# FiLM layer: the stores moved from ACT's DMA queue to SP's, behind the loads

## Chip, cores, metric

One core of a Trainium2 chip. The metric is device time in microseconds (us), lower is better. The span in a profile is about 1.8 us shorter than the time. Most executions agree within 0.3%; some are 1.5% to 5% longer, and these slow ones are left out of all comparisons. MB is 10^6 bytes, except in the profile's KB column.

## The reference

```python
# x: (32, 512, 256) f32, conditioning: (32, 64), gamma_proj and beta_proj: (64, 256)
gamma = conditioning @ gamma_proj
beta = conditioning @ beta_proj
return (x * (1 + gamma[:, None, :]) + beta[:, None, :]).astype(np.float32)
```

16.78 MB of x are read, 16.78 MB of output are written; the rest is small.

## The kernel before

x goes through SBUF in four slabs of 4.19 MB, each with its own buffer (nothing is ever reused, so no load waits for a store). Each slab is worked on in two groups of 16 rows per partition: 11 rows on VectorE, 5 on GpSimd, a multiplication and an addition each, in place. Each group is then stored, so there are eight stores, called S0 to S7 below.

```python
    LOADS = {0: [8, 24]}
    GROUP = 16
    ON_DVE = 11
    ...
    nc.scalar.dma_start(out=cond_s, in_=conditioning)
    nc.scalar.dma_start(out=gbproj[:, :dim], in_=gamma_proj)
    nc.scalar.dma_start(out=gbproj[:, dim:], in_=beta_proj)
    ...
    for s in range(SLABS):
        xs = xpool.tile([P, ROWS, dim], f32, name=f"xs{s}")
        ...
        for n in LOADS.get(s, [ROWS]):
            nc.sync.dma_start(out=xs[:, r : r + n, :], in_=x_v[s, :, r : r + n, :])
    ...                       # gamma and beta for each partition by matmuls: gb_p (PSUM), gb_s (SBUF)
    for s in range(SLABS):
        for r0 in range(0, ROWS, GROUP):
            ...
            nc.vector.scalar_tensor_tensor(out=v, in0=rows(g_p, nv), scalar=1.0, in1=v,
                                           op0=ALU.add, op1=ALU.mult)
            nc.gpsimd.tensor_tensor(out=w, in0=w, in1=rows(g_s, nw), op=ALU.mult)
            nc.vector.tensor_add(out=v, in0=v, in1=rows(b_p, nv))
            nc.gpsimd.tensor_tensor(out=w, in0=w, in1=rows(b_s, nw), op=ALU.add)
            nc.scalar.dma_start(out=o_v[s, :, r0 : r0 + GROUP, :],
                                in_=xs[:, r0 : r0 + GROUP, :])
```

## Time and profile before

| | before |
|---|---|
| time, median (range) | 84.53 us (84.4 to 85.89, 6 runs) |
| span of the profiled run | 82.6 us |
| bytes, mean rate over the span | 33.69 MB, 408 GB/s |
| VectorE / GpSimd busy | 60% / 56% |
| last VectorE instruction ends | 66.6 us |
| first store issued, last load landed | 25.9 us, 49.5 us |

The chain of work that ended last (shares of the span by engine):

```profile
DVE 49%; DMA 16%; issue 11%; PE 2%; ACTq 1%; ACT 1%
```

### The profile page before, as it was taken

What the parts mean: (1) busy time and instruction counts of PE and PEld (TensorE: products, weight loads), DVE (VectorE), ACT (ScalarE), POOL (GpSimd) and SP (SyncE); (2) the same over time, 40 slices, a digit from 0 to 9 for tenths busy, and PEclk for the clock granted to TensorE, in tenths of its full rate; (3) what the DMA queues carried; (4) which work ended last, traced back from release to release, by engine and by line L of the source; (5) the groups of instructions that cost most, each with busy time, mean ns of one, the idle gap of its engine ahead of it and who ended that gap; (6) DMA issues with size and microseconds to landing.
All of it is one profiled execution on the core that took longest, in us unless ns stands there. A gap on an engine that the chain in (4) does not pass through costs nothing.

```text
span 82.6 us, 156 instructions
## 1 busy us (share of the span) xinstructions
PE 9.1 (11%) x10; PEld 2.8 (3%) x10; DVE 49.9 (60%) x18; ACT 3.9 (5%) x9; POOL 46.2 (56%) x22
## 2 busy tenths in 40 slices
PE   0080000899600000000000000000000000000000
PEld 0100000443000000000000000000000000000000
DVE  2011000059999999999999999999999920000000
ACT  0600000034400000000000000000000000000000
POOL 2000000069999999999999999999995000000000
DMA  3899999969969989998889979899999999999992
GB/s 56 337 508 397 389 397 524 460 302 508 508 270 492 508 381 381 413 476 381 381 381 556 460 302 460 381 468 421 429 452 389 468 421 421 460 389 452 437 421 87
DMA packets 2080, 33.69 MB, mean 408 GB/s; under 512 B 288, under 2 KB 416, under 8 KB 416
## 3 DMA queue, kind: packets, MB, share of 16 engines
q1 hardware_dynamic: 720, 16.78, 48.6%
q10 hardware_dynamic: 1360, 16.92, 48.0%
HBM read 16.92 MB, written 16.78 MB: 408 GB/s over the span
## 4 chain that ended last, share of the span: by engine, by line
DVE 49%; DMA 16%; issue 11%; PE 2%; ACTq 1%; ACT 1%
DVE xs L100 30%; DVE xs L103 19%; DMA gbproj<-in_beta_proj_dram 16%; PE gb_p L79 2%; ACTq L50 1%; ACTq L48 0%; ACT gb_s L82 0%; ACT gb_s L85 0%
## 5 line engine op out<-in xcount | busy, mean ns | idle before, releaser
L102 POOL TENSOR_TENSOR xs<-xs,gb_s 128x1280 f32<-128x1280 f32 x8 | 23.0, 2895 | 16.2 <-ACT gb_s L82 16.2
L100 DVE SCALAR_TENSOR_TENSOR xs<-gb_p,xs 128x2816 f32<-128x2816 f32 x8 | 24.7, 3083 | 10.9 <-ACT gb_s L85 10.9
L103 DVE TENSOR_TENSOR xs<-xs,gb_p 128x2816 f32<-128x2816 f32 x8 | 24.7, 3086 | 0.3
L104 POOL TENSOR_TENSOR xs<-xs,gb_s 128x1280 f32<-128x1280 f32 x8 | 23.0, 2893 | 0.0
L79 PE MATMUL gb_p<-gbproj,cond_T 64*128 64x512 f32 x8 | 7.2, 1074 | 8.9 <-DMA gbproj<-in_beta_proj_dram 8.9
L74 DVE COPY cond_T<-cond_T_p 64x512 f32<-64x512 f32 x1 | 0.7, 683 | 4.3 <-PE cond_T_p L72 4.3
L79 PEld LDWEIGHTS gb_p<-gbproj,cond_T 64*128 64x128 f32 x8 | 2.5, 328 | 13.7 <-issue 13.7
L72 PE MATMUL cond_T_p<-rident,cond_s 32*64 32x512 f32 x2 | 1.9, 1065 | 3.9 <-DMA cond_s<-in_conditioning_dram 3.9
L82 ACT ACTIVATE gb_s<-gb_p 128x256 f32<-128x256 f32 x4 | 1.5, 383 | 16.4 <-PE gb_p L79 16.4
L85 ACT COPY gb_s<-gb_p 128x256 f32<-128x256 f32 x4 | 1.5, 367 | 0.0
L82 ACT ACT_TABLE_LOAD x1 | 1.3, 1283 | 2.4 <-issue 2.4
L67 DVE COPY rident<-ident 32x512 f32<-32x512 f32 x1 | 0.4, 416 | 1.2 <-POOL ident masks.py:199 1.2
L72 PEld LDWEIGHTS cond_T_p<-rident,cond_s 32*64 32x64 f32 x2 | 0.3, 202 | 3.9 <-issue 3.9
masks.py:197 POOL MEMSET ident<- 32x32 f32 x1 | 0.1, 114 | 0.3 <-POOLq L121 0.3
masks.py:199 POOL TENSOR_SCALAR_AFFINE_SELECT ident<-ident 32x32 f32<-32x32 f32 x1 | 0.2, 202 | 0.1
L121 POOL MEMSET const-float32-0.0<- 128x1 f32 x1 | 0.1, 103 | 0.2 <-issue 0.2
L121 POOL MEMSET const-bfloat16-1.0<- 128x1 bf16 x1 | 0.1, 106 | 0.0
L121 POOL MEMSET const-uint8-127<- 128x1 uint8 x1 | 0.1, 106 | 0.0
L121 POOL MEMSET const-float32-1.0<- 128x1 f32 x1 | 0.1, 103 | 0.0
## 6 DMA issues: line engine op xcount, KB each, us to landing
out_dram<-xs ACTq DMA_DIRECT2D x8, 2048.0 KB, 18.2
xs<-in_x_dram SPq DMA_DIRECT2D x3, 4096.0 KB, 32.9
xs<-in_x_dram SPq DMA_DIRECT2D x1, 3072.0 KB, 12.2
xs<-in_x_dram SPq DMA_DIRECT2D x1, 1024.0 KB, 4.6
gbproj<-in_gamma_proj_dram ACTq DMA_DIRECT2D x1, 64.0 KB, 9.1
gbproj<-in_beta_proj_dram ACTq DMA_DIRECT2D x1, 64.0 KB, 12.9
cond_s<-in_conditioning_dram ACTq DMA_DIRECT2D x1, 8.0 KB, 3.0
```

Source lines behind the costliest of these rows:

```text
L50: nc.scalar.dma_start(out=gbproj[:, :dim], in_=gamma_proj)
L67: nc.vector.tensor_copy(out=rident.rearrange("p (b g) -> p b g", g=REP), in_=ident.to_broadcast([batch, batch, REP]),)
L72: nc.tensor.matmul(cond_T_p, lhsT=cond_s, rhs=rident, start=True, stop=True)
L74: nc.vector.tensor_copy(out=cond_T, in_=cond_T_p)
L79: nc.tensor.matmul(p_t, lhsT=cond_T[:, s * P : (s + 1) * P], rhs=gbproj, start=True, stop=True)
L82: nc.scalar.activation(out=s_t[:, :dim], in_=p_t[:, :dim], func=mybir.ActivationFunctionType.Identity, bias=1.0, scale=1.0)
L85: nc.scalar.copy(out=s_t[:, dim:], in_=p_t[:, dim:])
L100: nc.vector.scalar_tensor_tensor(out=v, in0=rows(g_p, nv), scalar=1.0, in1=v, op0=ALU.add, op1=ALU.mult)
L102: nc.gpsimd.tensor_tensor(out=w, in0=w, in1=rows(g_s, nw), op=ALU.mult)
L103: nc.vector.tensor_add(out=v, in0=v, in1=rows(b_p, nv))
L104: nc.gpsimd.tensor_tensor(out=w, in0=w, in1=rows(b_s, nw), op=ALU.add)
L121: nc = _bacc.Bacc("TRN2", target_bir_lowering=False, num_devices=1)
```

## The change

Intent: loads first, stores after them, in one queue, so that the loads are never slowed by stores sharing their turns. In the profile SP's queue is q1 and ACT's is q10; a queue's part on one of the 16 DMA engines is called a ring below.

```diff
-            nc.scalar.dma_start(out=o_v[s, :, r0 : r0 + GROUP, :],
-                                in_=xs[:, r0 : r0 + GROUP, :])
+            nc.sync.dma_start(out=o_v[s, :, r0 : r0 + GROUP, :],
+                              in_=xs[:, r0 : r0 + GROUP, :])
```

## The prediction

> **What bounds the kernel now.** I read the page's slices first, because the kernel does two vector passes over 16.78 MB and must read and write each byte once, so the question is whether the DMA engines or VectorE set the end.
>
> ```profile
> DVE  2011000059999999999999999999999920000000
> POOL 2000000069999999999999999999995000000000
> DMA  3899999969969989998889979899999999999992
> DMA packets 2080, 33.69 MB, mean 408 GB/s; under 512 B 288, under 2 KB 416, under 8 KB 416
> q1 hardware_dynamic: 720, 16.78, 48.6%
> q10 hardware_dynamic: 1360, 16.92, 48.0%
> ```
>
> VectorE and GpSimd work without a gap in the middle of the span and stop with seven slices to go. The DMA row is at eight or nine tenths nearly everywhere from the second slice to the last but one. The two queue shares add to 96.6% of all 16 engines' time. By the sizes in the packet records, q1 holds the five loads of x (SP), and q10 the stores together with the three small loads of ACT (16.78 + 0.14 MB).
>
> The chain of work that ended last names VectorE for 49% of the span. That must not be read as the bound: it follows the last store back to the instruction that allowed it. What VectorE's pace is worth shows in the stretches (columns: window, its length, busy time of each engine with instruction counts, clock, DMA share, GB/s):
>
> ```profile
> 2.00:25.90 23.90, 9.09 (x10) 2.79 (x10) 9.03 (x4) 3.87 (x9) 8.60 (x4) 1.00 0.99 418
> 25.90:49.50 23.60, 0.00 (x0) 0.00 (x0) 23.46 (x9) 0.00 (x0) 23.60 (x10) 1.00 1.01 425
> 49.50:80.00 30.50, 0.00 (x0) 0.00 (x0) 16.98 (x6) 0.00 (x0) 13.47 (x5) 1.00 1.01 432
> ```
>
> I chose the borders from the issues: the first store is issued at 25.94 us, and the last load, issued at 10.3 us, lands 39.2 us later, at 49.5. So the first stretch carries loads only, the second both directions, the third stores only. All three move nearly the same, 418, 425 and 432 GB/s, with the engines' share at about 1. Transfers bind in all of them, whatever their direction. After VectorE's last instruction (63.49 + 3.09 = 66.58 us) there are still 16 us of stores: VectorE finished long before the data did.
>
> ```profile
> 63.49 3.09 DVE L103 TENSOR_TENSOR xs<-xs,gb_p 128x2816 f32<-128x2816 f32 x1
> L59 SPq DMA_DIRECT2D xs<-in_x_dram x5: 328/424/623, 0.7 to 10.3; - x5
> L105 ACTq DMA_DIRECT2D out_dram<-xs x8: 338/339/368, 25.9 to 66.7; - x8
> out_dram<-xs ACTq DMA_DIRECT2D x8, 2048.0 KB, 18.2
> ```
>
> A store takes 18.2 us (median) from issue to landing, though 2.10 MB at 432 GB/s need 4.85 us: stores already stand in a backlog, and the compute is not what they wait for.
>
> **What the Trainium skill says.** All from the page "DMA: Bandwidth & Descriptors". "Issuing engines are not separate DMA queues": transfers from any issuing engine run on the same 16 DMA engines, and using several saves only sequencer time. The before trace agrees in that SP's queue alone already gets 418 GB/s, and the two queues together only 425. "Queues, rings and completion order": SP and ACT each own one ring on each of the 16 engines, and an engine takes turns between rings packet by packet. The trace agrees in the split: by 25.9 us about 10.11 MB have moved (418 GB/s for 23.9 us, plus 0.116 MB in the first slice), so 16.92 - 10.11 = 6.81 MB of loads remained and took the 23.6 us to 49.5, that is 289 GB/s, leaving 425 - 289 = 136 for stores. This is 2.1 to 1; load packets are mostly 32 KB and store packets 16 KB in the records, so alternate turns give 2 to 1. "Where 436 GB/s comes from" puts the port ceiling at 435.2 GB/s. The stores-only stretch runs at 432, so nothing is left above it.
>
> **The change part by part.** The order of instructions of the built kernels is the same on PE, VectorE and GpSimd. The eight stores leave ACT and stand on SP behind all five loads.
>
> *Issue time.* Eight stores by 0.339 us = 2.7 us move from ACT to SP. ACT's last compute was at 22.2 us, and SP issues its last load long before 25.9, so both have idle time: 0 us on the path. The fifth load waited until 10.3 us before, for a semaphore shared with the gamma load; in the built kernel after, it shares none and should be issued by about 2.6 us. Four loads stood ahead of it in the queue anyway (8.4 MB not yet moved at 10.3 us is certain, since only some 3.6 MB had), so 0 us too.
>
> *Loads no longer share turns with stores.* From 25.9 us the remaining 6.81 MB of loads have the engines alone: 6.81 MB / 432 GB/s = 15.8 us, so the last load lands at 41.7 us, not 49.5. Nobody waits for it: VectorE has no gap before either. 0 us on the path by itself.
>
> *Stores wait behind the loads.* The first is issued at 25.9 us but moves from 41.7 us. Eight stores are 16.78 MB / 432 = 38.8 us, so the last byte moves at 80.5 us. For this to hold, each store must be ready when its turn comes. Store k (0 to 7) has its turn at 41.7 + 4.85 k; VectorE completes group k at about 23.73 + 6.12 k (L103 ends at 23.73 for the first, 66.58 for the last). Production is slower than the drain, so the slack shrinks; the last store has turn 75.7 against ready 66.6: 9.1 us remain. No bubble.
>
> *The sum.* Before, the same accounting gives 10.11 + 425 x 23.6 (10.03) + 432 x 30.5 (13.18) = 33.32 MB at 80.0, and 0.37 MB more, 0.86 us: transfer end at 80.9 us, span end at 82.6 (1.7 us for the last landing and the closing barrier). After: 80.5 + 1.7 = 82.2. The difference is 0.4 us, all from the mixed stretch (23.6 us at 425 becoming 432: 23.6 x 7/432 = 0.38). Applied to the median of 84.59: 84.2 us.
>
> **The rivals.**
>
> *One ring is slower than two.* If a ring left holes where one transfer follows another, or between loads and stores, two rings would hide them and one would not. A hole of 0.3 us at each of about 12 borders would cost 3.6 us: 87.8. Against it: the 2.00 to 25.90 stretch has one ring for x with several borders, and the stores-only stretch has ACT's ring alone with borders about every 5 us, and runs at 432. What 418 lacks of 432 in the first, 0.8 us, includes the start-up and the small packets of gamma and beta. I leave some tenths for the one new border between loads and stores.
>
> *Mixing the directions costs more than I see.* If separating reads from writes lifted the rate above 432, the time would fall: at 450 GB/s in everything after 25.9 us, 23.58 MB would take 52.4 instead of 54.6 us, or 82.0. For it speaks only that the mixed stretch is the lowest after start-up, and some of its slices are ragged. Against it: both pure stretches are before us, and neither exceeds 432.
>
> *The stores become paced by compute at the end.* They start 15 us late; if they then moved faster than data is made, the end would be VectorE's end plus one store: 66.6 + 4.85 + 1.7 = 73.2 us of span, 75 of time. That needs the bytes to move at far over 435 GB/s, which cannot be. The opposite form, idle DMA now that early stores are held back, needs a stretch with no loads left and no store ready; with three groups done or nearly done at 41.7 us (ready at 25.9, 29.9, 36.0), and 9 us of slack at the end, it does not occur.
>
> *SP blocked by a store's wait ahead of a load.* SP issues in order, so a load behind a store would starve VectorE. The order shows all five loads first and no load after them: excluded here.
>
> **Range and chances.** Centre 84.2. Down, the most I can credit is recovering the mixed stretch twice over, about 83.5. Up, some tenths for the turn from loads to stores and the scatter of before, whose three runs span 84.4 to 85.89: 85.2. Two per cent is 1.7 us, that is 82.9 or 86.3. A gain so large needs a rate above what any stretch shows: 0.02. A loss so large needs holes in a single ring: 0.03. Within 2%: 0.95.
>
> **What would show it.** In the profile after: q1 at 33.55 MB and about 96% of the engines, q10 at 0.14 MB; the last load landing near 41.7 us, 7 to 8 us earlier; the first store's landing 20 to 21 us after its issue, and the last one's about 14; VectorE still gapless and ending at 66.6 us; the rate between 26 and 80 us flat at 430 to 433, without a dip at 41.7. I would be wrong if the DMA row shows slices of seven or fewer after the first store (holes in the one ring), if pure stretches ran clearly over 435 GB/s, or if VectorE ended at a different time, which would mean that the loads' order mattered to compute after all.

## The result and the profile after

84.61 us median (84.46 to 88.66, 6 runs, the 88.66 a slow one) against 84.53. A ratio here and below is the mean time of one kernel's fast runs over that of the other's in the same rounds, so it is not quite the ratio of the medians. It is 1.0013, 95% interval 0.9995 to 1.0031: the same, within the range, and without the predicted gain of 0.4 us.

The slices and queues of the kernel after, to be held against those that the prediction shows of before:

```profile
DVE  2002000049999999999999999999999920000000
DMA  2899999889979989997969999999999999999991
q1 hardware_dynamic: 1872, 33.56, 95.8%
q10 hardware_dynamic: 208, 0.14, 0.5%
63.75 3.09 DVE L103 TENSOR_TENSOR xs<-xs,gb_p 128x2816 f32<-128x2816 f32 x1
```

All bulk bytes are now in SP's queue, at nearly the same total share of the 16 engines (96.3% against 96.6%). VectorE stands in the same slices; the last line is its last instruction, which ends at 66.84 us. The issues (min/median/max duration in ns, then first and last start in us) and their times to landing:

```profile
L59 SPq DMA_DIRECT2D xs<-in_x_dram x5: 382/428/667, 0.7 to 2.8; - x5
DMA to landing us min/median/max: 4.9/21.7/40.2
L105 SPq DMA_DIRECT2D out_dram<-xs x8: 332/333/348, 26.2 to 66.9; - x8
DMA to landing us min/median/max: 15.1/19.3/22.7
```

The last load is issued at 2.8 instead of 10.3 us and lands at 2.8 + 40.2 = 43.0 instead of 49.5. The first store is issued at 26.2 us (25.9 before), but lands 22.7 us later, since it stands behind the loads. The first stretch below holds loads only, the second the turn from loads to stores, the third stores only:

```profile
26.00:38.00 12.00, 0.00 (x0) 0.00 (x0) 11.93 (x5) 0.00 (x0) 12.00 (x6) 1.00 1.01 437
38.00:46.00 8.00, 0.00 (x0) 0.00 (x0) 7.93 (x4) 0.00 (x0) 8.00 (x3) 1.00 1.00 408
46.00:80.00 34.00, 0.00 (x0) 0.00 (x0) 20.73 (x7) 0.00 (x0) 17.20 (x7) 1.00 1.01 431
```

The turn looks weak. In a window of 8 us that alone is no proof: the 16 engines move nearly in step (the starts of one row lie within about 0.6 us), a row of 16 load packets of 32 KB is 0.5 MB, and the rate counted in a window depends on whether such a row falls in or out (hence the 437). So I went to the records of single packets. From 16 us on, outside the places named here, 32 KB load packets take 1.213 us and 16 KB store packets 0.611, in both kernels. (Before that, load packets stand beside the small ones of gamma and beta, and some are longer.) In the kernel after, the last row of load packets ahead of the first store takes 1.62 us on average (1.26 to 2.07), so 0.41 us are lost per engine on average. On each engine the first store packet starts the moment its last load packet ends, so there is no hole, only these long packets. In the kernel before, two rows are long, one just before S0's packets begin at 29.8 us (0.24 us lost) and one when S1's do (0.20 us). Between 36 and 48 us of the kernel before, where loads and stores alternate packet by packet, the packets take 1.213 and 0.611 us, as they do alone.

```profile
26.00:34.00 8.00, 0.00 (x0) 0.00 (x0) 7.93 (x4) 0.00 (x0) 8.00 (x3) 1.00 1.02 416
36.00:48.00 12.00, 0.00 (x0) 0.00 (x0) 11.93 (x4) 0.00 (x0) 12.00 (x5) 1.00 1.01 437
```

These two stretches of the kernel before agree: the weak part of the mixed time is where the stores start, not where the directions are mixed.

### The profile page after: what moved, and what is told of

The parts are those of the page before. It is cut to its first block, busy times and chain, and to the rows that moved or that the text cites. A ratio compares the mean times of both kernels' runs of the same rounds, so it can differ in the third digit from the quotient of the medians.

```text
span 82.8 us, 156 instructions
## 1 busy us (share of the span) xinstructions
PE 9.1 (11%) x10; PEld 2.8 (3%) x10; DVE 49.9 (60%) x18; ACT 3.9 (5%) x9; POOL 46.2 (56%) x22
## 4 chain that ended last, share of the span: by engine, by line
DVE 48%; DMA 16%; issue 11%; PE 2%; ACTq 1%; ACT 1%
DVE xs L100 30%; DVE xs L103 19%; DMA gbproj<-in_beta_proj_dram 16%; PE gb_p L79 2%; ACTq L50 1%; ACTq L48 0%; ACT gb_s L82 0%; ACT gb_s L85 0%
```

## The experiments

Theory: the bytes at the DMA engines' rate set the end; the queue and the order of the bytes do not matter while the engines always have a packet waiting and no store's data come late. The small expected gain is missing because a beginning of stores costs about 0.4 us in either kernel. The rivals: mixed directions cost something and the single ring takes it back; or the chain of waits is right and VectorE's pace counts.

All kernels are correct except e4. "First to last" is the time from the first packet of x to the end of the last store's packets; at 1.213 and 0.611 us per 32 and 16 KB packet and no loss it would be about 78 us. "Turn" is what the packets lost beside these durations where stores begin, as a mean over the engines. Both are from the packet records of the one profile that each run has, so how much they vary from execution to execution is known only roughly: after, e4, e7 and e8, which have the same load sizes in one queue, lose 0.41 to 0.57.

| run | time, median us | ratio to before (95%) | first to last | turn |
|---|---|---|---|---|
| before | 84.53 | | 79.65 | 0.24 + 0.20 |
| after | 84.61 | 1.0013 (0.9995 to 1.0031) | 79.87 | 0.41 |
| e1_loads2mb | 84.79 | 1.0027 (1.0005 to 1.0049) | 79.60 | 0.05 |
| e2_turns3 | 84.99 | 1.0051 (1.0029 to 1.0073) | 79.96 | 0.15 in all |
| e3_apart | 86.13 | 1.0189 (1.0166 to 1.0212) | 81.40 | hole of 2.0 |
| e4_noadd (wrong result) | 84.55 | 1.0004 (0.9983 to 1.0026) | 80.02 | 0.57 |
| e5_last16k | 84.67 | 1.0000 (0.9972 to 1.0027) | 79.86 | 0.37 |
| e6_before16k | 84.81 | 1.0016 (0.9988 to 1.0044) | slow profile | |
| e7_dve14 | 88.05 | 1.0402 (1.0367 to 1.0436) | 83.16 | 0.44 |
| e8_load_behind_s4 | 90.03 | 1.0620 (1.0576 to 1.0664) | 85.40 | 0.56 |
| e9_first16k | 84.50 | 0.9985 (0.9957 to 1.0013) | 79.85 | 0.36 |
| e10_8_24_16k | two fast runs, 84.81 and 84.95 | 1.0035 (1.0000 to 1.0070) | slow profile | |
| e11_before_all16k | 85.31 | 1.0123 (1.0056 to 1.0190) | 80.22 | 0.62 in all |
| e12_whole_slabs | 84.65 | 1.0008 (0.9984 to 1.0031) | 79.83 | none |

### e4: VectorE's half taken away

```diff
-            nc.vector.tensor_add(out=v, in0=v, in1=rows(b_p, nv))
-            nc.gpsimd.tensor_tensor(out=w, in0=w, in1=rows(b_s, nw), op=ALU.add)
```

> The kernel after without the two additions of beta: wrong result on purpose, half the vector work (VectorE ends near 42 us instead of 66.8). Theory 'bytes': 84.3 to 84.8 us, no change, because the stores wait for the loads until 41.7 us and then for one another. Rival 'the chain of waits is right and VectorE's 48% is the bound': some 20 us less.

Unchanged, as the theory has it. Rows of the page, VectorE, GpSimd and DMA:

```profile
DVE  2002000049999930998019980000000000000000
POOL 2000000059999900997019960000000000000000
DMA  2999999989979998997969999999999999999991
```

VectorE has half the work, waits for loads in between (7.4 us, so that it ends at 49.4 us and not near 42 as expected) and is done nine slices earlier; the DMA row and the end stay. Half of VectorE's work was worth nothing, although the chain of waits of the kernel after names it for 48%.

### e3: the same order of bytes by a semaphore wait

```diff
+            if s < 3:     # kernel before; stores on ACT
+                nc.scalar.activation(out=xs[:, r0, 0:1], in_=slabs[3][:, r0, 0:1],
+                                     func=mybir.ActivationFunctionType.Identity,
+                                     bias=xs[:, r0, 0:1], scale=0.0)
             nc.scalar.dma_start(out=o_v[s, :, r0 : r0 + GROUP, :],
```

> The kernel before (stores on ACT's own queue), with every store of the first three slabs held back by a one-element ACT operation that reads slab 3, so that no store is issued before the last load has landed (result unchanged: 0 times x3 plus x). The order of the bytes is that of the kernel after, but by a semaphore wait in place of a place in the queue. Theory 'queueing behind the loads is free because the next packets already stand in the ring': here the DMA engines idle from the last load's packet to the first store's, landing plus issue plus start, 2.5 to 3.5 us (in the kernel before the first store was issued at 25.94 us and its packets begin near 28.7), so 86.8 to 88.2 us. Rival 'separating the directions pays, and the single ring eats the gain': about 84.2, the hole being smaller than 0.5 us.

86.13 us: 1.5 us more than the kernel after. A hole, but 2.0 us instead of 2.5 to 3.5, so the expected time was missed by 0.7 us. Stretches of this run, then ACT at the turn:

```profile
41.00:42.00 1.00, 0.00 (x0) 0.00 (x0) 1.00 (x1) 0.00 (x0) 1.00 (x1) 1.00 0.15 66
42.00:43.00 1.00, 0.00 (x0) 0.00 (x0) 1.00 (x2) 0.21 (x2) 1.00 (x1) 1.00 0.01 0
43.00:44.00 1.00, 0.00 (x0) 0.00 (x0) 1.00 (x1) 0.27 (x2) 1.00 (x2) 1.00 0.00 0
44.00:80.00 36.00, 0.00 (x0) 0.00 (x0) 22.76 (x8) 1.07 (x4) 19.27 (x7) 1.00 1.01 433
...
42.79 0.48 ACT L106 ACTIVATE xs<-xs,xs 128x1 f32<-128x1 f32 x2 [19.88 <-DMA xs<-in_x_dram]
43.16 0.85 ACTq L109 DMA_DIRECT2D out_dram<-xs  x2
```

The loads' packets run out, the landing reaches ACT, ACT works and issues, and the rate is back. In the packet records 1.97 us lie, on average over the engines, between the last row of loads and the first of stores. My 2.5 to 3.5 came from the kernel before, from S0's issue at 25.94 us to its packets, and I took these to begin near 28.7; the records have 29.8. There load packets kept the engines busy in between, and here the first store packet starts 0.9 us after its issue at 43.16. So the time from issue to packet in the kernel before was no measure of the hole. Less the 0.41 us that the kernel after loses at its turn, the hole leaves 1.97 - 0.41 = 1.56 us, and first to last differs by 81.40 - 79.87 = 1.53. So what the change has over a wait is that the stores already stand in the ring when the loads end. The two rings as such neither help nor hurt.

### e7: where VectorE begins to count

```diff
-    ON_DVE = 11
+    ON_DVE = 14
```

> The kernel after with 14 of 16 rows on VectorE in place of 11, so that VectorE's chain lasts 14/11 as long and ends near 80.2 us, past the 75.7 us at which the last store has its turn. By the slack worked out (9 us) this is 4.5 us too much: the last store moves from about 81.3 to 86.2, span 87.9, time 89 to 90.5. Rival 'bytes alone': 84.6. Rival 'VectorE's time counts in full': 13.4 us more, 98.

88.05 us, 1 us below the expected range, between the two rivals. The VectorE instruction grew from 3083 to 3884 ns, not to the 3924 that 14/11 gives, since part of it does not grow with the rows; VectorE ended at 78.96 us, not 80.2.

```profile
26.00:66.00 40.00, 0.00 (x0) 0.00 (x0) 39.93 (x11) 0.00 (x0) 12.11 (x10) 1.00 1.01 427
66.00:86.00 20.00, 0.00 (x0) 0.00 (x0) 12.93 (x4) 0.00 (x0) 0.00 (x0) 1.00 0.75 322
```

Up to 66 us the DMA engines are full; then they are 0.75 busy, for want of data. VectorE ended 78.96 - 66.84 = 12.1 us later than in the kernel after, the time rose by 88.05 - 84.61 = 3.4, so 8.7 us were slack, against 9.1 in the prediction. The expected time was too long by about what VectorE ended too early.

### e8: a load behind a store that waits

```diff
-            nc.sync.dma_start(out=xs[:, r : r + n, :], in_=x_v[s, :, r : r + n, :])
+            if s < 3:
+                nc.sync.dma_start(out=xs[:, r : r + n, :], in_=x_v[s, :, r : r + n, :])
...
                               in_=xs[:, r0 : r0 + GROUP, :])
+            if s == 2 and r0 == 0:
+                nc.sync.dma_start(out=slabs[3], in_=x_v[3])
```

> The kernel after with the load of slab 3 issued behind the fifth store (S4) in SP's queue instead of ahead of all stores. SP issues in order, so this load goes out only when S4's data are ready, about 49.5 us, and moves behind S0 to S4, 56 to 66 us, landing near 67; VectorE stands idle from 54.8 to 67 us and ends near 79.5; the DMA engines idle from 71 to 76.5 us. Time 89.5 to 91. Rival 'the order in the queue is free as long as the bytes are the same': 84.6.

90.03 us, inside the range. Its waits (us in total, times, longest) and two stretches:

```profile
DVE xs L101 <- DMA xs<-in_x_dram: 13.4, 1, 13.4
...
56.00:66.00 10.00, 0.00 (x0) 0.00 (x0) 0.00 (x0) 0.00 (x0) 0.00 (x0) 1.00 1.06 454
71.00:76.00 5.00, 0.00 (x0) 0.00 (x0) 5.00 (x2) 0.00 (x0) 5.00 (x2) 1.00 0.09 36
```

VectorE waits 13.4 us for the late load; while it makes up for it, the DMA engines stand empty for 5 us. So one queue is not harmless whatever its order: here a load that VectorE needed stood behind a store that was waiting for data. (In e2 below two loads stand behind waiting stores as well, but they land before they are needed; VectorE waits for no load there.)

### e1 and e2: more turns in the one ring

e1 is the kernel after with all loads in 2 MB pieces, still ahead of the stores. e2 has the same pieces, and the last two are issued behind S0 and S1.

```diff
-    LOADS = {0: [8, 24]}
+    LOADS = {s: [16, 16] for s in range(4)}      # e1 and e2
...
                               in_=xs[:, r0 : r0 + GROUP, :])
+            if s == 0:                           # e2 alone; slab 3 not loaded above
+                nc.sync.dma_start(out=slabs[3][:, r0 : r0 + GROUP, :],
+                                  in_=x_v[3, :, r0 : r0 + GROUP, :])
```

> Control for the next run: the kernel after with every load cut to 2 MB (16 rows), all still ahead of the stores on SP. Theory 'bytes at 432 GB/s, plus about 0.4 us once where stores begin': 84.2 to 84.8 us, one dip in the rate at about 41 us. Rival 'each border between transfers in one ring leaves a hole': 8 loads in place of 5, so some 3 holes more, above 85 us if a hole is 0.3 us.

> The same 2 MB loads, but the last two are issued behind the first and the second store, so that the one ring turns from loads to stores three times in place of once (L6 S1 ... order: six loads, S0, L6, S1, L7, S2 and on). No compute starves: load 7 should land near 51.5 us and is needed at 54. Theory 'each turn from loads to stores costs every engine 0.4 us': 0.8 us over the control, about 85.3, with three dips in the rate at about 32, 42 and 51 us. Rival 'the cost falls only once, at the first store of the program': same as the control within 0.2 us, one dip at 32 us.

84.79 us, inside its range, and 84.99 us, nearer to the rival. Three turns in place of one cost 0.2 us in the medians, with the two intervals overlapping, and 0.15 us of long packets in all. First to last is 0.36 us longer, but not at the turns: in e2 the engines finish less evenly (on average 0.46 us before the last one, in e1 0.11). So "each turn costs 0.4 us" is refuted in this setting; borders inside the ring leave no holes either (e1 has three more, and first to last is 79.60). But e1 has hardly any loss at its single turn and is no faster: its start loses about 0.3 us more in long packets, with 16 KB packets between the small ones of gamma and beta.

### e5, e6, e9, e10, e12: what the long packets at the turn depend on

All change only LOADS: e5 `{0: [8, 24], 3: [16, 16]}`, e9 `{0: [16, 16]}`, e10 `{0: [8, 24]}` and `[16, 16]` for the others, e12 `{}` (whole slabs), all in the kernel after; e6 `{0: [8, 24], 2: [16, 16], 3: [16, 16]}` in the kernel before.

> The kernel after with the last slab's load cut into two of 2 MB, so that the packets just ahead of the stores are 16 KB and not 32 KB. In the trace after, the last row of 32 KB packets ahead of the stores took 1.62 us on average against 1.213 elsewhere, 0.41 us lost per engine. In the run with all loads cut to 2 MB this loss was 0.05. Theory 'the loss goes with 32 KB load packets where a store begins': loss below 0.1, time 84.1 to 84.5, ratio to before near 0.998. Rival 'the loss is the turn's own and only shows elsewhere when packets are small': 84.6, unchanged.

> The kernel before with the loads of the last two slabs cut into two of 2 MB each: its two weak rows of packets (1.46 and 1.41 us instead of 1.213, at the first and second store, 0.44 us in sum) fall on these loads. Theory 'first stores beside 32 KB load packets cost it': the rows disappear, the stretch from 26 to 49 us moves 430 to 432 GB/s in place of 425, time 84.1 to 84.5. Rival 'mixing the directions itself costs the 0.4 us': the stretch stays at 424 to 426 and the time at 84.5 to 84.7.

> The kernel after with only the first slab's load cut otherwise, 16 and 16 rows in place of 8 and 24; slabs 1 to 3 stay whole (32 KB packets). What is open: the row of long packets at the turn (0.41 us) was there in the kernel after and with the last slab in 16 KB packets, and not with all loads in 16 KB packets. Theory 'it follows from how the first slab is cut, which sets how the engines stand to one another': no such row here, under 0.1 us. Rival 'it follows from 32 KB packets anywhere ahead in the ring': 0.3 to 0.5 us, as in the kernel after. Time 84.3 to 84.8 in either case.

> The counterpart: 8 and 24 rows for the first slab, 16 and 16 for all the others. Theory 'first slab': 0.3 to 0.5 us lost at the turn. Rival '32 KB packets': under 0.1 us. Time 84.3 to 84.8 in either case.

> The kernel after with four whole-slab loads, no small first one. The only place where more than some tenths are left is the start: about 0.7 us are lost beside full rate between 2 and 14 us, with 8 KB packets first and the small gamma and beta packets between. 'Fewer, larger packets at the start win': 84.1 to 84.4. 'It is the start itself and the small loads': 84.5 to 84.8. VectorE waits for beta until 17.5 us and should not notice the later first load.

e5 loses 0.37 us at the turn although 16 KB packets stand there, so the size of the packet just ahead is not the cause. e9 loses 0.36 us with the first slab cut evenly, so it is not the cut of the first slab. e12 has 32 KB packets alone and loses nothing at the turn, so 32 KB packets are not sufficient. Each of my explanations fell. e6 and e10 were profiled slow, so their packets say nothing; their times show no gain. e12 gives back at the start what it saves at the turn (0.4 us more lost in the first 18 us), so its time is the same as well. I leave open what makes the packets long: it is not any one of the sizes that I changed. One pattern stands in the table that no run here tests: with everything in one queue, the profiles whose loads all have one packet size lose little (e1 0.05, e2 0.15, e12 none), and those with several sizes lose 0.36 to 0.57 (after, e4, e5, e7, e8, e9). e10 would have tested it, but its profile is slow; e11, with one size and two queues, loses 0.62.

### e11: mixed directions without 32 KB packets

The loads of e1 in the kernel before.

```diff
-    LOADS = {0: [8, 24]}
+    LOADS = {s: [16, 16] for s in range(4)}
```

> The kernel before (two queues, directions mixed) with all loads cut to 2 MB, as in the first control. 'Bytes': 84.4 to 84.9 us, as that control on one queue (84.79). 'Mixing costs': the mixed stretch at 424 to 426 GB/s and 0.4 us more than the control, 85.2. 'The cost sits at the first stores': 430 to 432 GB/s once two stores have started.

85.31 us, above the 84.4 to 84.9 of "bytes" and near the 85.2 of "mixing costs". The edit also delays loads: SP waits for earlier transfers, and the last load is issued at 23.4 us (8.8 in e1); VectorE waits 2.2 us for loads, but the packet records show no idle time of the DMA engines from 4 to 80 us. The stretches decide between the last two (first stores, mixed, stores only):

```profile
23.00:30.00 7.00, 0.00 (x0) 0.00 (x0) 7.00 (x4) 0.00 (x0) 6.92 (x4) 1.00 1.01 396
30.00:48.00 18.00, 0.00 (x0) 0.00 (x0) 17.93 (x6) 0.00 (x0) 17.76 (x7) 1.00 1.00 429
48.00:80.00 32.00, 0.00 (x0) 0.00 (x0) 15.26 (x5) 0.00 (x0) 12.84 (x5) 1.00 1.01 432
```

Once the first store is under way, mixed traffic runs at 429 GB/s, nearly what stores alone get. Its 0.62 us at the first stores, in the packet records, against 0.05 in e1, are of about the size of the difference to e1 in first to last (80.22 - 79.60 = 0.62). So the loss sits at the first stores, in this profile as in that of the kernel before.

No version beats both kernels; e9, at 0.9985, does not exclude 1.

## Why the prediction was right, and where a step was not

- **The bound, and the main claim (same time): right.** First to last is 79.65 us before and 79.87 after. e4, made from the kernel after, shows that VectorE does not bind, e3 that a hole in the DMA does show in the time.
- **Issue time and order: right.** The stores cost SP 0.333 us each at a time when it has nothing else to do. The last load is issued at 2.8 us (predicted 2.6). No compute engine waits for it in either kernel.
- **No bubble among the stores: right**, with the slack measured by e7 as 8.7 us against 9.1.
- **The step that failed: "The difference is 0.4 us, all from the mixed stretch (23.6 us at 425 becoming 432".** The rate was read as a property of mixing and carried over to all 23.6 us. In the packet records mixing costs nothing; the loss was 0.44 us in two rows of packets at S0 and S1. The change moved it to 42 us as one row of 0.41. The term should have been 0.44 - 0.41 = 0.03 us. First to last differs by 0.2 the other way. In the packet records all long packets together lose 1.22 us per engine before and 1.21 after; the 0.2 is idle time at the two ends, where the engines start and finish less evenly (they finish on average 0.18 us before the last one in the profile before, 0.32 after). With one profile of each, this is not shown to be the change's doing. The prediction allowed "some tenths for the one new border between loads and stores" in its range; in the sum it belonged to the centre. Also, 425 against 432 over 23.6 us is 0.17 MB, less than one row of packets (0.5 MB): the view could not carry the number; that it came near the 0.44 was luck.
- **Landing times: 1.3 to 1.7 us short.** Predicted 41.7 for the last load, 20 to 21 for the first store and 14 for the last; measured 43.0, 22.7 and 15.1. I had worked out when the bytes move, and a landing is reported later (the last load's packets end at 42.1 to 42.7 us); the 0.41 us at the turn is in it too. In the sum it did not matter, since the same tail stood on both sides. Its size was off: the last packets end at 81.4 us before and 81.6 after, which leaves 1.2 us to the end of the span, not 1.7.
- **Its own signs of being wrong.** The "slices of seven or fewer after the first store" came: the DMA row after has a 7 and a 6 there (37 to 39 and 41 to 43 us). They are not the holes that the prediction meant: in the packet records the engines stand idle for less than 0.03 us in any 2 us between 4 and 80 us. The sign was badly chosen, since the row of the kernel before has a 7 at 48 us too. The rate was not flat either: 408 GB/s from 38 to 46 us, where the long packets are. VectorE has no gap, but ends at 66.84 and not 66.6 us, because beta landed 0.25 us later.
- **The rivals:** "one ring is slower than two" is refuted by e1 and e2; "SP blocked by a store's wait ahead of a load" was rightly excluded for this order, and e8 shows what it costs where the order allows it. e2 shows that such a load does not always starve VectorE.

## What to carry to other kernels

When the DMA engines are full from beginning to end, as here, the queue in which a transfer stands moves waiting about and not the end; look for the slack between each store's turn and its data (here 9 us) before counting on either side. Queueing stores behind loads in one ring was free with every load issued ahead of every store; doing the same by a semaphore wait cost 1.5 us. A load behind a store that must wait cost 5.4 us where VectorE came to wait for it (e8), and about 0.2 beside e1 where it did not (e2). A rate difference read from a window counts only if it is worth more bytes than one row of packets at its edges.

## What the Trainium skill lacked or had wrong

- "DMA: Bandwidth & Descriptors", section "Where 436 GB/s comes from", says that for transfers between HBM and SBUF the HBM side (about 358 GB/s) binds. For this kernel on one core that does not hold: loads and stores ran at 431 to 433 GB/s over tens of microseconds, near the 435 that the same section gives for the ports. The section itself calls a measured 425 GB/s near that rate, so its sentence lacks the condition under which it is true.
- The same page, section "Issuing engines are not separate DMA queues", is confirmed in its main point (84.53 against 84.61 us), but that section has no number for handing over from one transfer to the next. (The page's fixed cost of about 2.0 us for a DMA, in "Anatomy of one DMA", is for those issued from GpSimd.) Here: within one ring, or at packet level between two, no hole; by landing, semaphore and a new issue from ACT, 1.97 us.
- No page that I read has the cost where stores begin beside or behind loads: 0.36 to 0.62 us per program in most fast profiles, 0.15, 0.05 and none in three (e2, e1, e12), cause open.
